# Bringing the solved 32x32 blocks back through DRAM in one load of 2 KB rows

## The chip, the cores and the metric

The kernel runs on one core of one Trainium2 chip. The metric is device time in microseconds (us). Three runs of the kernel before gave a median of 1629.85 us (1623.73 to 1634.08); a profiled execution stands beside them.

## The reference, cut to what matters

One layer of a decoder trunk is applied to a new sequence of 2048 positions and to 8 short samples of 8 positions. One input projection (1024 columns in) feeds two branches of 512 columns each, and one output projection joins them:

```
xn = rms_norm(x, norm_g);  p = xn @ w_in
conv branch : u = C*h;  z = 3-tap causal conv of u;  out = B * z * silu(G)
rwkv branch : per head (8 heads of 64), per token
    sa = S (-kk)
    S  = S * diag(w) + sa (kk*a)^T + v k^T
    o  = S r          then GroupNorm, + bonus, * silu(gate)
y = concat(conv, rwkv) @ w_out;  result = rms_norm(x + y)
```

The recurrence is computed in chunks of 64 positions. Inside a chunk the tokens depend on each other through a strictly triangular 64x64 matrix A, so each chunk and head needs (I - A)^-1. That inverse is the part this case is about.

## The kernel before, in words

**The outer loop.** Two halves of the sequence (`hf` 0 and 1, 1024 positions each; the samples ride with half 0) times four head pairs give eight passes, `s` = 0 to 7 (lines 925 to 956); I call them pair 0 to pair 7. One pass works on 128 partitions: two heads of 64. In program order a pass is `rwkv_pair` (four projection columns and the making of the recurrence's operands), `inverse`, `wkv` (16 chunks in order, with the group norm behind each block of 4, 6 and 6 chunks), and `conv_group` (four projection columns of the conv branch). Pass 3 differs: there `conv_group` and `xprep(1)`, which normalises and transposes the second half of the input, stand in the program ahead of `inverse` and `wkv` (lines 950 to 954).

**The order of the work.** No order is written by hand. Every tile is asked for by a tag, and tiles of one tag share a fixed number of buffers. When the kernel is compiled, a planner takes the operations in program order as their priority, puts each on its engine's queue as soon as its operands and its buffer are there by the planner's own durations, and fills the rest of each engine with later operations that are ready. The order on each engine is then fixed; on the chip an engine waits at its next instruction until its semaphores are there. So the projection matmuls (`pj`) of the conv group and of the next pair fill TensorE between the small matmuls of the recurrence.

**The inverse.** `rwkv_pair` leaves A in tile `AB`, `AB[128, chunks, 128]`, one tile for each of the three blocks. `store_blocks` (line 624) writes the diagonal 32x32 blocks to DRAM (`dn`), and `inverse` (line 636) reads them back as `na` with one block (head h, half b, chunk c) on a partition, twice: partitions 0 to 63 solve the even columns of each inverse block, 64 to 127 the odd ones. The tile `x` holds the columns, 16 a partition, 32 long. It has tag `xi`, one buffer, and is set to the identity by three memsets on GpSimd (lines 640 to 643). `subst` (line 610) solves on VectorE in 31 steps of two operations. Then `x` goes to DRAM (`dx`) in two stores (line 665), and comes back as matrices with 32 rows on partitions: for each of the three blocks, four loads (two heads by two diagonal blocks, line 674) write straight into the diagonal blocks of `AB`. Store and load move runs of 32 floats, 128 bytes. For each block the off-diagonal part follows (lines 676 to 690): a transpose on VectorE, small matmuls into `cx`, a copy split over ScalarE and VectorE, small matmuls again, and a copy into `AB`. After that `wkv` reads `AB` as an operand of its chunks (`ca`, `oo`).

**The tag `c2`.** It has four buffers of 2 KB a partition and serves short uses: in `sample_chunk` the state `s0` that is loaded from an input (line 803, passes 0 to 3) and four temporaries, in `wkv` the output block `ob`, in `gn_out` the tile `yo` that is stored to DRAM, and in `xprep(1)` the discarded output of the eight sums of squares on ScalarE (line 247, one for each of eight row tiles of the input).

**Queues.** SyncE (SP) issues the stores and loads of `dn`, `na`, `dx`, `AB`, of `yd` and of the weights in half 0; GpSimd's queue issues the weights in half 1 (`wh<-wsp`, `wl<-wsp`).

Of the kernel before, what the change touches and what calls it, by code (L numbers as in the profile page):

```python
# [8 lines left out]
F32 = mybir.dt.float32  # L9
# [78 lines left out]
def trunk_kernel(ctx, tc, I, O):  # L88
    nc = tc.nc
    act, dve, pe, pool, sync = nc.scalar, nc.vector, nc.tensor, nc.gpsimd, nc.sync  # L90
# [5 lines left out]
    dram = ctx.enter_context(tc.tile_pool(name="dram", bufs=1, space=DRAM))  # L96
    cnt = [0]

    def T(pool, shape, tag, bufs=1, dt=F32):
        cnt[0] += 1  # L100
        return pools[pool].tile(shape, dt, tag=tag, bufs=bufs, name=f"{tag}_{cnt[0]}")
# [8 lines left out]
    def CX(shape):  # L110
        return PS(shape, "cx", 1)
# [4 lines left out]
    def copy(out, in_, scale=1.0, bias=0.0):  # L116
        act.activation(out=out, in_=in_, func=AF.Copy, scale=scale, bias=bias)  # L117
# [7 lines left out]
    def mul(out, in0, in1):  # L125
        tt(out, in0, in1, ALU.mult)

    def mm(out, lhsT, rhs, start=True, stop=True):
        pe.matmul(out, lhsT=lhsT, rhs=rhs, start=start, stop=stop)  # L129
# [53 lines left out]
    for p in range(NPAIR):  # L183
        t = T("const", [128, 64], f"sst{p}")
# [425 lines left out]
    def subst(na, x, n, par):  # L610

        rows = na.shape[0]
        cw = x.shape[1]
        for s in range(n - 1):
            w = min(s // par + 1, cw)
            m = n - 1 - s
            t = T("small", [128, 144], "sub", 1)[:rows, :w * m].rearrange("p (c t) -> p c t", t=m)
            mul(t, x[:, 0:w, s:s + 1].to_broadcast([rows, w, m]),
                na[:, s, s + 1:n].unsqueeze(1).to_broadcast([rows, w, m]))
            tt(x[:, 0:w, s + 1:n], x[:, 0:w, s + 1:n], t, ALU.add)  # L620
            if s % 4 == 3:
                yield
# [13 lines left out]
    def inverse(S):  # L636
        cb = S.cb
        na = T("pair", [128, 32, 32], "na", 1)
        x = T("pair", [128, 16, 32], "xi", 1)
        pool.memset(x, 0.0)  # L640
        xf = x.rearrange("p c t -> p (c t)")
        for q in range(2):
            pool.memset(xf[q * 64:q * 64 + 64, q::34], 1.0)
        for q in range(2):
            sync.dma_start(out=na[q * 64:q * 64 + 64], in_=S.dn.rearrange("h b c s t -> (h b c) s t"))
        if cb:
            ab = S.AB[0][:, 0, 0:64]
            dd = T("small", [128, 8], "dd", 1)
            dve.tensor_reduce(out=dd, in_=ab.rearrange("p (b t) -> p t b", t=8), axis=mybir.AxisListType.X, op=ALU.add)
            nas = T("small", [16, 8, 8], "nas", 1)  # L650
            sync.dma_start(out=nas, in_=dd)
            xs_ = T("small", [16, 8, 8], "xis", 1)
            pool.memset(xs_, 0.0)
            pool.memset(xs_.rearrange("p c t -> p (c t)")[:, 0::9], 1.0)
            yield from subst(nas, xs_, 8, 1)
            d2 = T("small", [128, 8], "dd", 1)
            sync.dma_start(out=d2, in_=xs_)
            mul(ab.rearrange("p (b t) -> p b t", t=8), d2.unsqueeze(1).to_broadcast([128, 8, 8]),
                bmask.unsqueeze(2).to_broadcast([128, 8, 8]))
        yield from subst(na, x, 32, 2)  # L660
        yield
        cnt[0] += 1
        dx = dram.tile([2, 2, 16, 16, 2, 32], F32, tag="dx", bufs=2, name=f"dx_{cnt[0]}")
        for q in range(2):
            sync.dma_start(out=dx[:, :, :, :, q, :].rearrange("h b c s t -> (h b c) s t"), in_=x[q * 64:q * 64 + 64])
        ty = T("pair", [128, 2, 16, 32], "na", 1)
        t1, ys = ty[:, 0], ty[:, 1]
        for bl in S.bls:
            AB, n, c0_ = S.AB[bl.i], bl.nch, bl.ch0
            e = 1 if bl.samp else 0  # L670
            for h in range(2):
                for b in range(2):
                    r = h * 64 + b * 32
                    sync.dma_start(out=AB[r:r + 32, e:e + n, b * 32:b * 32 + 32],
                                   in_=dx[h, b, c0_:c0_ + n].rearrange("c s q t -> (s q) c t"))
            dve.transpose(out=t1[:, c0_:c0_ + n, :], in_=AB[:, e:e + n, 0:32])
            py = CX([128, n, 32])
            for c in range(n):
                for h in range(2):
                    a, b = h * 64, h * 64 + 32  # L680
                    mm(py[b:b + 32, c, :], AB[a:a + 32, e + c, 32:64], t1[a:a + 32, c0_ + c, :])
            copy(ys[32:64, c0_:c0_ + n], py[32:64])
            dve.tensor_copy(out=ys[96:128, c0_:c0_ + n], in_=py[96:128])
            pt = CX([128, n, 32])
            for c in range(n):
                for h in range(2):
                    a, b = h * 64, h * 64 + 32
                    mm(pt[a:a + 32, c, :], ys[b:b + 32, c0_ + c, :], AB[b:b + 32, e + c, 32:64])
            copy(AB[0:32, e:e + n, 32:64], pt[0:32])
            dve.tensor_copy(out=AB[64:96, e:e + n, 32:64], in_=pt[64:96])  # L690

# [234 lines left out]
    for s in range(8):  # L926
# [23 lines left out]
        if s == 3:  # L950
            run(conv_group(xs, hf, p))
            xs = xprep(1)
        run(inverse(S))
        wkv(S)
        if s != 3:
# [4 lines left out]
    for hf in range(2):  # L960
        for bl in half_blocks(hf):
            e = SAMP if bl.samp else 0
            for i in range(bl.np // 128):
                t = slice(hf * HALF + bl.p0 + i * 128, hf * HALF + bl.p0 + (i + 1) * 128)
# [58 lines left out]
```

## Time and profile before

| what | before |
|---|---|
| median of three runs | 1629.85 us (1623.73 to 1634.08) |
| the profiled execution | 1627.34 us, of it 1625.4 us from the first to the last instruction |
| busy | TensorE 93%, its weight loads 78%, VectorE 62%, ScalarE 38%, GpSimd 18% |
| mean granted clock of TensorE | 0.966 |
| DMA packets | 121967, of them 62617 under 512 bytes |
| chain that ended last | TensorE 63%, VectorE 22%, DMA 6% |

Busy shares are averages over the span; a matmul's end is modelled, so a busy TensorE is not one at its peak. The chain of waits is followed back from the last instruction: at each step to what released it, or to the instruction before it on its engine. The granted clock is 1.00 at 2.4 GHz and 0.50 at 1.2 GHz; a mean between them is a mixture of the two.

### The profile page before, as it was taken

What the parts mean: (1) busy time and instruction counts of PE and PEld (TensorE: products, weight loads), DVE (VectorE), ACT (ScalarE), POOL (GpSimd) and SP (SyncE); (2) the same over time, 40 slices, a digit from 0 to 9 for tenths busy, and PEclk for the clock granted to TensorE, in tenths of its full rate; (3) what the DMA queues carried; (4) which work ended last, traced back from release to release, by engine and by line L of the source; (5) the groups of instructions that cost most, each with busy time, mean ns of one, the idle gap of its engine ahead of it and who ended that gap; (6) DMA issues with size and microseconds to landing.
All of it is one profiled execution on the core that took longest, in us unless ns stands there. A gap on an engine that the chain in (4) does not pass through costs nothing.

```text
span 1625.4 us, 29341 instructions
## 1 busy us (share of the span) xinstructions
PE 1517.5 (93%) x11088; PEld 1267.9 (78%) x11088; DVE 1011.9 (62%) x3101; ACT 616.3 (38%) x1591; POOL 290.4 (18%) x395
## 2 busy tenths in 40 slices
PE   4999999989999999879999899999998999899997
PEld 4988877877788778867789678977896788667885
DVE  7387458655687458775587258635863587466544
ACT  6452345324532354344451245134413533342221
POOL 3133103311133112320022002200220022000000
PEclk9999999899999998989999899999999999899999
DMA  7323412242043213341123212321241135414441
GB/s 239 117 83 126 122 44 96 84 121 81 19 131 112 94 49 113 124 137 60 36 62 109 67 35 63 108 68 36 61 124 53 36 100 158 144 61 136 141 138 52
DMA packets 121967, 151.90 MB, mean 93 GB/s; under 512 B 62617, under 2 KB 86681, under 8 KB 121826
## 3 DMA queue, kind: packets, MB, share of 16 engines
q1 hardware_dynamic: 107024, 104.53, 20.9%
q0 software_dynamic: 9536, 34.64, 6.7%
q10 hardware_dynamic: 5266, 10.86, 1.8%
q8 instruction: 88, 1.44, 0.4%
q14 instruction: 53, 0.43, 0.1%
HBM read 92.60 MB, written 57.35 MB: 92 GB/s over the span
## 4 chain that ended last, share of the span: by engine, by line
PE 63%; DVE 22%; DMA 6%; issue 5%; ACT 3%; SPq 1%; POOL 1%; ACTq 0%; DVEq 0%; POOLq 0%
PE pj L129 41%; PE ca L129 5%; PE ax L129 5%; DVE sub L123 5%; DVE xi L123 4%; PE cb L129 4%; PE oo L129 2%; DVE hp L123 2%; PE cx L129 2%; PE cx L699 1%; DMA hp<-in_x_prompt 1%; DMA dx<-xi 1%; DVE hp L120 1%; DMA AB<-dx 1%; DMA na<-dn 1%
## 5 line engine op out<-in xcount | busy, mean ns | idle before, releaser
L129 PE MATMUL pj<-xh,wh 128*128 128x384 f32 (+3 forms) x1856 | 654.8, 353 | 17.4 <-DVE hp L123 13.7
L129 PE MATMUL pj<-xl,wh 128*128 128x384 f32 (+3 forms) x1856 | 652.6, 352 | 2.6 <-POOL xl L207 1.9
L129 PE MATMUL pj<-xh,wl 128*128 128x384 f32 (+3 forms) x1856 | 652.0, 351 | 0.6 <-DMA wl<-wsp 0.6
L129 PEld LDWEIGHTS pj<-xh,wh 128*128 128x128 f32 x1856 | 356.3, 192 | 50.1 <-DVE hp L123 11.2
L129 PEld LDWEIGHTS pj<-xl,wh 128*128 128x128 f32 x1856 | 356.8, 192 | 31.4 <-POOL xl L207 2.8
L129 PEld LDWEIGHTS pj<-xh,wl 128*128 128x128 f32 x1856 | 355.4, 191 | 28.1 <-issue 2.0
L117 ACT ACTIVATE tS<-sv,wc 64x64 f32<-64x64 f32 x256 | 88.0, 344 | 118.7 <-DVE sv L120 95.6
L207 POOL TENSOR_TENSOR wl<-wr,wh 128x512 fp32r<-128x512 f32 x66 | 87.6, 1338 | 195.1 <-ACT wh L117 191.7
L120 DVE SCALAR_TENSOR_TENSOR sv<-cb,wc,tS 64x64 f32<-64x64 f32 x240 | 68.0, 283 | 62.7 <-PE cb L129 55.0
L129 PE MATMUL ax<-L,bk 64*128 64x128 f32 x528 | 79.4, 299 | 21.0 <-DVE bk L123 12.7
L129 PEld LDWEIGHTS ax<-L,bk 64*128 64x128 f32 x528 | 66.3, 198 | 38.0 <-issue 23.2
L123 DVE TENSOR_TENSOR sub<-xi,na 128x126 f32<-128x126 f32 (+22 forms) x248 | 79.8, 322 | 16.3 <-DMA na<-dn 9.2
L117 ACT ACTIVATE t<-pj,prm 128x384 f32<-128x384 f32 (+3 forms) x170 | 68.9, 433 | 53.5 <-PE pj L129 52.4
L747 DVE TENSOR_SCALAR u<-ca,Q 128x64 f32<-128x64 f32 x128 | 36.2, 283 | 81.2 <-PE ca L129 81.0
L527 POOL TENSOR_TENSOR bk<-t,t 64x384 f32<-64x384 f32 (+2 forms) x56 | 58.0, 1036 | 144.4 <-ACT t L499 78.3
L123 DVE TENSOR_TENSOR xi<-xi,sub 128x126 f32<-128x126 f32 (+22 forms) x248 | 76.8, 310 | 7.3
L117 ACT ACTIVATE wh<-wr 128x512 fp32r<-128x512 f32 x66 | 40.5, 625 | 94.6 <-PE pj L129 74.5
L129 PEld LDWEIGHTS ca<-sv,L 128*64 128x64 f32 x528 | 43.7, 134 | 38.1 <-DVE sv L120 13.8
L737 DVE COPY xs<-ca 128x64 f32<-128x64 f32 x128 | 28.7, 224 | 66.2 <-PE ca L129 57.0
L129 PE MATMUL ca<-sv,L 128*64 128x64 f32 x528 | 68.7, 245 | 0.1
L294 POOL DMA_DIRECT2D wh<-wsp x33 | 18.7, 567 | 273.9 <-PE pj L129 199.6
L123 DVE TENSOR_TENSOR hp<-pj,hp 128x512 f32<-128x512 f32 (+1 forms) x34 | 23.4, 689 | 62.7 <-PE pj L129 62.3
(203 smaller groups left out, 2064.7 us busy)
## 6 DMA issues: line engine op xcount, KB each, us to landing
wr<-in_w_in SPq DMA_DIRECT2D x66, 256.0 KB, 3.7
wsp<-wh SPq DMA_DIRECT2D x33, 512.0 KB, 2.9
wsp<-wl SPq DMA_DIRECT2D x33, 512.0 KB, 3.9
wh<-wsp POOLq DMA_DIRECT2D x33, 512.0 KB, 3.6
wl<-wsp POOLq DMA_DIRECT2D x33, 512.0 KB, 4.5
hp<-in_x_prompt SPq DMA_DIRECT2D x29, 512.0 KB, 4.0
la<-yd SPq DMA_DIRECT2D x16, 512.0 KB, 4.0
out_y_p<-hp ACTq DMA_DIRECT2D x16, 512.0 KB, 2.6
```

The lines of the kernel that those rows point to most:

```text
L117: act.activation(out=out, in_=in_, func=AF.Copy, scale=scale, bias=bias)
L120: eng.scalar_tensor_tensor(out=out, in0=in0, scalar=scalar, in1=in1, op0=op0, op1=op1)
L123: dve.tensor_tensor(out=out, in0=in0, in1=in1, op=op)
L129: pe.matmul(out, lhsT=lhsT, rhs=rhs, start=start, stop=stop)
L207: eng.tensor_tensor(out=lo, in0=src, in1=hi.bitcast(F32), op=ALU.subtract)
L294: pool.dma_start(out=wh, in_=wsp[col, 0])
L527: pool.tensor_tensor(out=S.bk[bl.i][hs, chs, h, :], in0=ta[hs, a:a + n].rearrange("p (c j) -> p c j", j=64), in1=wi[hs, a:a + n].rearrange ...
L699: pe.transpose(out=pb[:, i, :], in_=S.bk[bi][:, ca + i].rearrange("p a t -> p (a t)"), identity=ident)
L737: dve.tensor_copy(out=xs_, in_=px)
L747: dve.tensor_scalar(out=u, in0=pu, scalar1=S.Q[:, q:q + 1], scalar2=None, op0=ALU.mult)
```

## The change

The solved columns are stored with another order of the axes, `[h, b, s, q, c, t]` in place of `[h, b, c, s, q, t]`, so that a row of the inverse is 16 chunks of 32 floats, 2 KB in one piece. The store is eight DMAs of 16 partitions each. One load brings all blocks of the pair into a new tile `xd` (tag `xd`, one buffer, the size of the old `xi`). Transposes and matmuls read `xd`; GpSimd and ScalarE copy the diagonal blocks from it into `AB`, two copies each for each block. The tile `x`, which had the tag `xi`, now takes one of the four buffers of `c2`.

```
     def inverse(S):
         cb = S.cb
         na = T("pair", [128, 32, 32], "na", 1)
-        x = T("pair", [128, 16, 32], "xi", 1)
+        x = T("ch", [128, 16, 32], "c2", 4)
...
-        dx = dram.tile([2, 2, 16, 16, 2, 32], F32, tag="dx", bufs=2, name=f"dx_{cnt[0]}")
+        dx = dram.tile([2, 2, 16, 2, 16, 32], F32, tag="dx", bufs=2, name=f"dx_{cnt[0]}")
         for q in range(2):
-            sync.dma_start(out=dx[:, :, :, :, q, :].rearrange("h b c s t -> (h b c) s t"), in_=x[q * 64:q * 64 + 64])
+            for h in range(2):
+                for b in range(2):
+                    u = q * 64 + (h * 2 + b) * 16
+                    sync.dma_start(out=dx[h, b, :, q].rearrange("s c t -> c s t"), in_=x[u:u + 16])
+        xd = T("pair", [128, 16, 32], "xd")
+        sync.dma_start(out=xd, in_=dx.rearrange("h b s q c t -> (h b s q) c t"))
...
-            for h in range(2):
-                for b in range(2):
-                    r = h * 64 + b * 32
-                    sync.dma_start(out=AB[r:r + 32, e:e + n, b * 32:b * 32 + 32],
-                                   in_=dx[h, b, c0_:c0_ + n].rearrange("c s q t -> (s q) c t"))
-            dve.transpose(out=t1[:, c0_:c0_ + n, :], in_=AB[:, e:e + n, 0:32])
+            cs = slice(c0_, c0_ + n)
+            dve.transpose(out=t1[:, cs, :], in_=xd[:, cs, :])
...
-                    mm(pt[a:a + 32, c, :], ys[b:b + 32, c0_ + c, :], AB[b:b + 32, e + c, 32:64])
+                    mm(pt[a:a + 32, c, :], ys[b:b + 32, c0_ + c, :], xd[b:b + 32, c0_ + c, :])
+            for h in range(2):
+                a = h * 64
+                pool.tensor_copy(out=AB[a:a + 32, e:e + n, 0:32], in_=xd[a:a + 32, cs, :])
+                copy(AB[a + 32:a + 64, e:e + n, 32:64], xd[a + 32:a + 64, cs, :])
             copy(AB[0:32, e:e + n, 32:64], pt[0:32])
             dve.tensor_copy(out=AB[64:96, e:e + n, 32:64], in_=pt[64:96])
```

## Rows read from the trace of the kernel before

**Rows 1.** The page: busy time of each engine, and the chain that ended last.
```profile
PE 1517.5 (93%) x11088; PEld 1267.9 (78%) x11088; DVE 1011.9 (62%) x3101; ACT 616.3 (38%) x1591; POOL 290.4 (18%) x395
...
PE 63%; DVE 22%; DMA 6%; issue 5%; ACT 3%; SPq 1%; POOL 1%; ACTq 0%; DVEq 0%; POOLq 0%
```

**Rows 2.** Windows: stretch, length, busy time by engine, granted clock, DMA share, GB/s.
```profile
1052.00:1212.00 160.00, 153.79 (x1224) 130.97 (x1223) 95.88 (x309) 57.54 (x157) 25.41 (x42) 0.97 0.24 69
700.00:720.00 20.00, 13.39 (x136) 11.55 (x136) 11.31 (x28) 10.36 (x19) 4.11 (x4) 0.83 0.73 195
720.00:760.00 40.00, 36.19 (x326) 28.47 (x326) 25.60 (x59) 22.61 (x63) 5.72 (x6) 0.91 0.13 41
760.00:823.00 63.00, 62.53 (x526) 48.42 (x526) 35.34 (x152) 29.32 (x88) 4.14 (x9) 1.00 0.13 40
890.00:921.00 31.00, 25.18 (x239) 21.53 (x238) 6.50 (x17) 6.41 (x20) 3.58 (x8) 0.78 0.32 77
```

**Rows 3.** Timeline of SP, pair 0: start us, length us, line, transfer, count.
```profile
164.75 1.30 SPq L665 DMA_DIRECT2D dx<-xi  x2
...
169.14 7.11 SPq L674 DMA_DIRECT2D AB<-dx  x12
```

**Rows 4.** Timeline of SP, pair 4.
```profile
889.85 1.26 SPq L665 DMA_DIRECT2D dx<-xi  x2
...
894.22 8.89 SPq L674 DMA_DIRECT2D AB<-dx  x12
```

**Rows 5.** Timeline of VectorE: the first transpose of pair 0 and of pair 4.
```profile
171.95 0.31 DVE L676 STREAM_TRANSPOSE na<-AB 128x128 f32<-128x128 f32 x1
...
901.79 0.31 DVE L676 STREAM_TRANSPOSE na<-AB 128x128 f32<-128x128 f32 x1 [0.49 <-DMA AB<-dx]
```

**Rows 6.** Waits of TensorE and GpSimd: who for whom, us in total, times, longest.
```profile
PE cx L129 <- DVE na L676: 17.4, 7, 5.8
...
POOL xi L640 <- DMA dx<-xi: 57.4, 5, 13.7
```

**Rows 7.** Instructions on tile AB: duration ns min/median/max, first and last start, forms.
```profile
L674 SPq DMA_DIRECT2D AB<-dx x96: 302/439/1920, 169.1 to 1388.0; - x96
...
L550 POOL TENSOR_TENSOR AB<-AB,Q x44: 288/507/617, 92.1 to 1338.6; 128x192 f32<-128x192 f32 x32, 128x256 f32<-128x256 f32 x8, 128x64 f32<-128x64 f32 x4
...
L117 ACT ACTIVATE AB<-cx x24: 254/319/322, 174.1 to 1398.7; 32x192 f32<-32x192 f32 x16, 32x128 f32<-32x128 f32 x8
```

**Rows 8.** The page: DMA issues, count, size of one, median us from issue to landing.
```profile
wr<-in_w_in SPq DMA_DIRECT2D x66, 256.0 KB, 3.7
...
dx<-xi SPq DMA_DIRECT2D x16, 128.0 KB, 3.5
...
AB<-dx SPq DMA_DIRECT2D x64, 24.0 KB, 2.0
```

**Rows 9.** Timeline of VectorE: the last write into c2 in pair 2.
```profile
628.37 0.59 DVE L120 SCALAR_TENSOR_TENSOR c<-c,prm,sg 128x384 f32<-128x384 f32 x1
```

**Rows 10.** Timeline of ScalarE: first and eighth square of xprep(1), the state's load of pair 3.
```profile
668.12 1.04 ACT L247 ACTIVATE c<-hp 128x1024 bf16<-128x1024 f32 x1
...
719.42 1.05 ACT L247 ACTIVATE c<-hp 128x1024 bf16<-128x1024 f32 x1
719.98 0.34 ACTq L803 DMA_DIRECT2D c<-in_state_wkv  x1
```

**Rows 11.** Groups of VectorE from 662 to 700 us: the solve of pair 3.
```profile
L123 DVE TENSOR_TENSOR xi<-xi,sub 128x126 f32<-128x126 f32 (+22 forms) x31 | 8.7, 280 | 0.8
L123 DVE TENSOR_TENSOR sub<-xi,na 128x126 f32<-128x126 f32 (+22 forms) x31 | 7.9, 254 | 0.8
```

**Rows 12.** Timeline of SP: the stores of the solved columns of pair 3.
```profile
699.10 1.29 SPq L665 DMA_DIRECT2D dx<-xi  x2
```

**Rows 13.** Timeline of VectorE: first chunk of pairs 0 and 3, last norm of pair 3.
```profile
196.56 0.28 DVE L747 TENSOR_SCALAR u<-ca,Q 128x64 f32<-128x64 f32 x1 [0.71 <-PE ca L129]
...
751.00 0.28 DVE L747 TENSOR_SCALAR u<-ca,Q 128x64 f32<-128x64 f32 x1 [0.69 <-PE ca L129]
...
822.90 0.62 DVE L120 SCALAR_TENSOR_TENSOR c<-c,prm,sg 128x384 f32<-128x384 f32 x1
```

**Rows 14.** Windows of the projection matmuls (pj) on TensorE alone: busy time, clock, DMA.
```profile
700.00:720.00 20.00, 6.20 (x48) 0.83 0.73 195
720.00:760.00 40.00, 23.03 (x87) 0.91 0.13 41
760.00:823.00 63.00, 42.49 (x189) 1.00 0.13 40
```

## The prediction, made before the changed kernel ran

> **What bounds the kernel now.** I read the page first. TensorE is busy 93% of the span, and the chain that ended last runs 63% over TensorE, 22% over VectorE and 6% over DMA [rows 1]. The windows say how these belong together: one whole period of half 1, from the stores of pair 5 to those of pair 6, lasts 160 us and TensorE is busy in 153.8 of them [rows 2]. Inside a period the recurrence is one serial chain (solve, DRAM, off-diagonal part, sixteen chunks, next pair's operands), and projection matmuls fill TensorE beside it. So a shortcut in the chain gains only what TensorE stands idle for, and a delay in the chain costs nothing until the filling runs out.
>
> The changed stretch shows where it is idle. In pair 0 the stores are issued at 164.75 us and the first transpose starts at 171.95, 7.2 us later [rows 3, 5]; in pair 4 it takes 11.9 us, from 889.85 to 901.79 [rows 4, 5]. The order on TensorE's queue is fixed, so where data come later than planned it stands: 17.4 us in 7 waits for the transposes, the longest 5.8 us [rows 6]. After that longest one the clock falls too, to a mean of 0.78 over 31 us [rows 2], which is 0.22 x 31 = 6.8 us of full-clock time. In quiet passes the stop is short or nothing.
>
> **The change part by part.**
>
> *Stores and load.* Before, SP issues 2 stores and 12 loads a pair. Afterwards it issues 8 stores and 1 load. A small transfer costs SP a median of 0.44 us [rows 7], but with the gaps 12 take 7.11 us or 0.59 each in pair 0 [rows 3]; I take 0.47 for a store (bounds 0.30 and 0.59). The eighth is issued 7 x 0.47 = 3.3 us behind the first and lands 2.0 us later, as the small loads do [rows 8], so 5.3 us after the first. The bounds are 2.1 + 2.0 and 4.1 + 3.5 (the big stores' landing). The load has the shape of a weight load, 256 KB in 2 KB rows, median 3.7 us to landing [rows 8]. Transposes can start at about 5.3 + 3.7 = 9.0 us. That is 1.8 us later than pair 0's 7.2 and 2.9 us earlier than pair 4's 11.9. What comes sooner is the second and third block: all three land together. But the three share one PSUM buffer (`cx`) and go one after the other anyway, so this helps only where a later load was late.
>
> By the Trainium skill (DMA: Bandwidth & Descriptors, "Anatomy of one DMA") a transfer takes about 2.0 us fixed plus its bytes at 436 GB/s, fitted on GpSimd's queue. For this load that is an estimate of 2.6 us where the row has 3.7; by it every operand would come 1.1 us sooner, up to 9 us over eight pairs.
>
> The loaded passes 4 to 6 gain at most the 17.4 us of waiting and the clock behind it, the quiet ones lose up to 1.8 us each. How the planner places the small matmuls anew the trace cannot show. If it moves them with the data, the stops vanish (17 us gained, and up to 7 more for the clock); if it leaves them where they are, all eight pairs stop for about 2 to 3 us, some 20 us in place of 17.4, with a part of the clock loss in the quiet passes too. I take +4 us; bounds -24 and +14. The value is near the second end, because the plan was short of the real transfers in the loaded passes before [rows 6] and SP's issue of eight stores is added ahead of the load.
>
> *SP's queue.* It is past the pair's transfers about 3 us sooner. Behind them wait stores of `yd`, a small weight tile and, in half 0, weights; TensorE does not wait for these by the list of waits, so nothing is gained.
>
> *Copies into AB.* Per block two on ScalarE, 32x192 like the copy from `cx`, 0.32 us each [rows 7]: 24 x 2 x 0.32 = 15 us of an engine that is 38% busy. They wait for the load alone and can go while TensorE makes the first product. If ScalarE takes them just ahead of the copy that TensorE waits for, 0.64 us a block come into the chain, at most 15 us in all if nothing covers them. The two on GpSimd are no longer than its 0.51 us for four times the partitions [rows 7]; the chunks that need them come more than 10 us later. I take 0.
>
> *The buffer of x.* The wait of GpSimd for the old `xi` buffer goes, 57.4 us in 5 waits [rows 6]. GpSimd is 18% busy, and behind its memset stand splits and weight DMAs of which TensorE waits for almost none: 0. What takes its place is more serious. `x` now queues for `c2`. I read from the trace that buffers of a tag are given in program order: pair 3's load of `s0`, which needs nothing but a free `c2` buffer, is issued at 719.98 us, right behind the eighth square of `xprep(1)` at 719.42 [rows 10], although after pair 2's last `yo` at 628.37 [rows 9] no one uses `c2` until the first square at 668.12. In pass 3 `xprep(1)` stands ahead of `inverse`, so there `x` has to come behind the eight squares as well. In the other passes what stands ahead of `x` is the previous pair's last `yo`, which ends before the next solve can begin: no cost.
>
> Before, pair 3's solve (62 operations, 16.6 us of VectorE) lay between 662 and 700 us [rows 11], its stores at 699.10 [rows 12]. It now starts at about 720 and lasts about 24 us beside the rest of `xprep(1)`: the stores go out at 744, **45 us later**. Not all of it arrives. Stores to first chunk took 31.8 us in pair 0 and 51.9 in pair 3 [rows 3, 12, 13], where `xprep(1)` lay in between; afterwards I take 32 + 2 = 34, so the first chunk is at 778 and not at 751.00, 27 us later. From there to the last norm it took 72 us [rows 13], with a projection matmul under way for 42.5 of 62.5 busy us of TensorE from 760 to 823 [rows 14, 2]. 324 projection matmuls ran from 700 to 823; three columns of pair 4, 216 of them, need nothing of pair 3's recurrence and will have gone ahead, so the chunks queue behind fewer. I take 10 us off (bounds 0 and 20) and 3 for the shorter remainder of pair 4: **+14 us**, bounds 0 and 30. It is a loss because TensorE, idle some 7 of 20 us from 700 to 720 already [rows 2], runs out of filling in that stretch.
>
> *Sum.* Against the profiled execution, 1627.3 us (2.5 below the median): 1627.3 + 14 + 4 + 0 = **1645 us**.
>
> **The rivals.**
>
> *A: the transfers decide (faster).* The 96 loads of 128-byte runs are what makes pairs 4 to 6 late, and one load of long rows ends that; the planner puts the matmuls where the data are, and pair 3 is covered by pair 4's projections. Gain: 17.4 us of stops, 6.8 us of clock in pair 4, 0.03 x 160 = 4.8 us in the period from pair 5 and the same again in pair 6 [rows 2, 6], 34 us at most; with the bulk of it 1602 us. For it: 11.9 against 7.2 us. Against it: the same two trips through DRAM remain, and the order of buffers.
>
> *B: no change.* Pair 4's columns and `xprep(1)` fill TensorE while pair 3 waits, and the stops move rather than go: 1627 us, give or take 9. For it: TensorE at 153.8 of 160 us. It decides if more than the 216 independent matmuls can go ahead; `v` and the gate of pair 4 write tiles that pair 3's chunks still read, which speaks against it.
>
> *C: the wait in pair 3 comes through whole.* Of the 45 us nothing is caught up behind the chunks, and the clock falls beside a half-empty TensorE: 1627 + 45 = 1672 us. Against it: 20 of them lay in `xprep(1)` already.
>
> *D: the planner takes `x` ahead of the squares.* Then the term of 14 is 0, and the result is A or B.
>
> **How the numbers follow.** Chances: my sum 0.57 (1634 to 1662), B 0.24, A 0.12, C 0.07; D is inside A and B. A change of 1%, 16 us, is about what a measurement of this kernel tells from no change, so the edges are 1614 and 1646, and my sum sits at the upper one. Of its 0.57 a little over 0.3 lie beyond, as its upper bounds are further off; with C that is 0.42 slower by over 1%. Faster is A, 0.12. Within 1% remain 0.46. The range from 1616 to 1668 leaves out A (0.12) and the end of C.
>
> **What would show it.** Right: in the trace afterwards pair 3's solve stands behind the eighth square, at about 720 us, its store near 744, and its first chunk near 778; pairs 0 to 2 make their first transpose about 9 us after the first store, and all three blocks' data are there at once; the waits of TensorE for transposes stay in the teens. Wrong: the solve of pair 3 ends near 700 as before (then D), or its delay is there and pair 4's stores are not later than before (then B); or the stops of pairs 4 to 6 and the low clock behind them are gone, with the span below 1614 (then A).

## The result, and the profile after

The changed kernel takes **1638.09 us** (median of 20 runs, 1629.73 to 1645.91); the kernel before, beside it, 1626.51 (20 runs, 1612.72 to 1636.12). The ratio is 1.0073, with a 95% interval of 1.0055 to 1.0091: slower, by less than 1%. The forecast was 1645. The profiled execution of after took 1632.51 us, 1630.7 of it span. All ratios here are of fast executions, and stage times are read from one profiled execution each, which in ring_alone below was a slow one and in half1_and_ring and two_stores_four_loads lies 17 and 11 us under the median.

The page of after, as [rows 1]: busy time by engine, and the chain that ended last.

```profile
PE 1528.8 (94%) x11088; PEld 1275.0 (78%) x11088; DVE 996.8 (61%) x3101; ACT 637.4 (39%) x1639; POOL 301.9 (19%) x443
...
PE 73%; DVE 16%; issue 4%; DMA 4%; ACT 2%; POOL 1%; SPq 0%; DVEq 0%; POOLq 0%; ACTq 0%
```

These averages hide nearly everything. I cut both spans at two points of the chain, the first store of the solved columns of pair 2 and that of pair 4, and counted for each stage, from all matmul and clock records, TensorE's time without a matmul and half of its time at 1.2 GHz, which is what a TensorE that is busy throughout loses by the lower clock (us, the last three columns after less before):

| stage | before | after | length | idle | half of the time at 1.2 GHz |
|---|---|---|---|---|---|
| start to pair 2's store | 517.9 | 533.1 | +15.2 | +3.7 | +10.2 |
| pair 2's to pair 4's store | 371.9 | 405.1 | +33.2 | +11.6 | +35.8 |
| pair 4's store to the end | 735.5 | 692.5 | -43.0 | -21.2 | -19.6 |
| sum | 1625.3 | 1630.7 | +5.4 | | |

So the change costs 48 us in one part and gives 43 back in another. The windows of half 1, first in the kernel before, from pair 4's store to the end (columns as in [rows 2]):

```profile
889.80:1625.30 735.50, 694.53 (x5026) 565.96 (x5025) 430.70 (x1384) 247.93 (x645) 82.44 (x125) 0.96 0.29 88
```

and after: one period, from pair 5's store to pair 6's, which answers to the 160.00 us of [rows 2]; then the same stage whole; last the stretch of pair 3's chunks.

```profile
1091.40:1240.20 148.80, 146.69 (x1212) 124.41 (x1211) 91.55 (x309) 60.36 (x164) 27.95 (x49) 1.00 0.25 73
938.20:1630.60 692.40, 672.74 (x5004) 547.61 (x5002) 417.04 (x1381) 257.49 (x667) 90.30 (x147) 0.99 0.31 93
788.60:850.00 61.40, 50.37 (x390) 33.40 (x383) 22.69 (x83) 19.50 (x60) 1.41 (x2) 0.50 0.02 8
```

The period is 11 us shorter, at a clock of 1.00. The wait of TensorE for transposes, 17.4 us in [rows 6] and 15.8 of them in half 1, is gone there: its longest waits from 938 us to the end of after are these (who for whom, us, times, longest).

```profile
PE pj L129 <- DVE t L120: 1.9, 2, 1.0
PE pj L129 <- DVE xl L207: 1.7, 2, 1.6
```

The stops did not go because the data come sooner. In pair 4 of after the first transpose starts 13.9 us after the first store, where it was 11.9 before [rows 4, 5], and in pairs 5 to 7 it is 16.1, 12.9 and 19.4 us where it was 8.9, 10.7 and 7.3:

```profile
938.17 4.06 SPq L668 DMA_DIRECT2D dx<-c  x8
...
952.11 0.82 DVE L677 STREAM_TRANSPOSE na<-xd 128x128 f32<-128x128 f32 x3
```

In between TensorE runs 97 projection matmuls without a gap, where before it ran 45 and stood for 5.8 us. After, then before (columns: PE, clock, DMA share, GB/s; of `pj` alone):

```profile
938.20:952.60 14.40, 14.40 (x97) 1.00 0.69 197
```

```profile
889.90:902.30 12.40, 6.43 (x45) 0.95 0.61 146
```

In pair 3 it goes the other way. ScalarE, GpSimd's queue of work, VectorE and SP of after, as [rows 10 to 13]: the eighth square, the load of `s0`, the memset of `x`, the solve's first operation, the stores and the first chunk.

```profile
732.36 1.05 ACT L247 ACTIVATE c<-hp 128x1024 bf16<-128x1024 f32 x1
...
734.65 0.33 ACTq L808 DMA_DIRECT2D c<-in_state_wkv  x1
```

```profile
728.06 0.53 POOL L640 MEMSET c<- 128x512 f32 x1
...
733.24 0.18 DVE L123 TENSOR_TENSOR sub<-c,na 128x31 f32<-128x31 f32 x1
...
765.76 3.79 SPq L668 DMA_DIRECT2D dx<-c  x8
...
810.38 0.28 DVE L752 TENSOR_SCALAR u<-ca,Q 128x64 f32<-128x64 f32 x1 [1.65 <-PE ca L129]
```

The memset at 728.06 shows that `x` had its buffer 4.3 us ahead of the eighth square; it does not wait for that square itself. The solve starts at 733 and not at 676 us, the stores go out at 765.8 and not at 699.1 [rows 12], the first chunk comes at 810.4 and not at 751.0 [rows 13]. Of the projection matmuls, which filled the chunks of pair 3 before (189 from 760 to 823), the windows of tile `pj` of after have 28 left for the stretch at 0.50, and more than before in pair 4's chunks (373 in 109.9 us against 289 in 103.4). After, then before (columns: PE, PEld, DVE, ACT, clock, DMA share, GB/s; of `pj` alone):

```profile
788.60:850.00 61.40, 14.06 (x28) 7.47 (x28) 1.10 (x2) 0.58 (x1) 0.50 0.02 8
938.20:1048.10 109.90, 75.54 (x373) 56.91 (x372) 7.26 (x13) 9.43 (x23) 1.00 0.21 64
```

```profile
760.00:823.00 63.00, 42.49 (x189) 29.20 (x189) 3.90 (x7) 5.33 (x14) 1.00 0.13 40
889.80:993.20 103.40, 65.81 (x289) 48.05 (x289) 7.27 (x13) 7.86 (x20) 0.93 0.19 50
```

In half 0 the new path is late. SP's timeline in pair 0 of after, as [rows 3], and VectorE's, as [rows 5]:

```profile
163.34 4.05 SPq L668 DMA_DIRECT2D dx<-c  x8
167.50 4.44 SPq L380 DMA_DIRECT2D yd<-hp  x3
172.03 0.38 SPq L435 DMA_DIRECT2D t<-in_w_da  x1
172.58 0.33 SPq L670 DMA_DIRECT2D xd<-dx  x1
```

```profile
177.90 0.62 DVE L120 SCALAR_TENSOR_TENSOR hp<-pj,omm,t 128x384 f32<-128x384 f32 x1 [3.47 <-ACT t L117]
178.44 0.82 DVE L677 STREAM_TRANSPOSE na<-xd 128x128 f32<-128x128 f32 x3
```

All three transposes stand together, 15.1 us after the first store (7.2 before). The load stands behind three stores of `yd`, and the transposes behind an operation on a projection, which waits for ScalarE: the planner has placed projections first. At the end of such a period TensorE's queue has no projection between 457.73 us and the first matmul on the next pair's operands, and TensorE stands until VectorE has made these; the next projections stand behind them in the queue. TensorE's timeline near 458 us in pair 1, where the granted clock is 0.50 for 17.1 us from 460.9:

```profile
457.73 0.33 PE L129 MATMUL pj<-xl,wh 128*128 128x384 f32 x1
461.59 0.76 PE L129 MATMUL ax<-L,bk 64*128 64x128 f32 x2 [3.54 <-DVE nwag L120]
...
463.14 0.69 PE L129 MATMUL pj<-xh,wl 128*128 128x384 f32 x1
```

Before, the longest stop ahead of such matmuls (`ax`) between the stores of pairs 0 and 3 was 1.5 us.

### The profile page after: what moved, and what is told of

Same layout as the page of the kernel before. It is cut to its first block, busy times and chain, and to the rows that moved or that the text cites. A ratio compares the mean times of both kernels' runs of the same rounds, so it can differ in the third digit from the quotient of the medians.

```text
span 1630.7 us, 29273 instructions
## 1 busy us (share of the span) xinstructions
PE 1528.8 (94%) x11088; PEld 1275.0 (78%) x11088; DVE 996.8 (61%) x3101; ACT 637.4 (39%) x1639; POOL 301.9 (19%) x443
## 3 DMA queue, kind: packets, MB, share of 16 engines
q1 hardware_dynamic: 91024, 104.53, 20.5%
## 4 chain that ended last, share of the span: by engine, by line
PE 73%; DVE 16%; issue 4%; DMA 4%; ACT 2%; POOL 1%; SPq 0%; DVEq 0%; POOLq 0%; ACTq 0%
PE pj L129 48%; PE ax L129 7%; PE ca L129 5%; PE cb L129 4%; DVE sub L123 3%; DVE c L123 3%; PE oo L129 2%; PE cx L129 2%; DMA na<-dn 2%; DVE hp L123 1%; PE cx L704 1%; DMA hp<-in_x_prompt 1%; DVE hp L120 1%; DVE bk L123 1%; PE cx L716 1%
## 5 line engine op out<-in xcount | busy, mean ns | idle before, releaser
L527 POOL TENSOR_TENSOR bk<-t,t 64x384 f32<-64x384 f32 (+2 forms) x56 | 53.3, 953 | 347.7 <-PE cb L129 105.5
L129 PE MATMUL ax<-L,bk 64*128 64x128 f32 x528 | 89.5, 317 | 21.5 <-DVE bk L123 7.9
L129 PEld LDWEIGHTS ax<-L,bk 64*128 64x128 f32 x528 | 71.2, 210 | 41.4 <-issue 25.6
L123 DVE TENSOR_TENSOR sub<-c,na 128x126 f32<-128x126 f32 (+22 forms) x248 | 78.9, 318 | 19.3 <-DMA na<-dn 12.2
L123 DVE TENSOR_TENSOR c<-c,sub 128x126 f32<-128x126 f32 (+22 forms) x248 | 75.0, 303 | 7.1
L120 DVE SCALAR_TENSOR_TENSOR hp<-pj,omm,t 128x384 f32<-128x384 f32 (+2 forms) x56 | 29.0, 529 | 76.6 <-ACT t L117 76.4
L129 PEld LDWEIGHTS ca<-sv,L 128*64 128x64 f32 x528 | 43.0, 140 | 40.7 <-DVE sv L120 15.2
L123 DVE TENSOR_TENSOR AB<-ax,msk 64x384 f32<-64x384 f32 (+2 forms) x88 | 48.7, 554 | 23.9 <-PE ax L129 22.7
```

What stands on the lines that cost most here:

```text
L120: eng.scalar_tensor_tensor(out=out, in0=in0, scalar=scalar, in1=in1, op0=op0, op1=op1)
L123: dve.tensor_tensor(out=out, in0=in0, in1=in1, op=op)
L527: pool.tensor_tensor(out=S.bk[bl.i][hs, chs, h, :], in0=ta[hs, a:a + n].rearrange("p (c j) -> p c j", j=64), in1=wi[hs, a:a + n].rearrange ...
```

## The experiments

A word on names: the **ring** is the four buffers of tag `c2`; the **path** is the new way through DRAM (stores, one load into `xd`, copies). Ratios are to the kernel before, run beside it.

**The path without the ring.** `xd` and `x` share the old single buffer.

```
-        x = T("ch", [128, 16, 32], "c2", 4)
+        x = T("pair", [128, 16, 32], "xi", 1)
...
-        xd = T("pair", [128, 16, 32], "xd")
+        xd = T("pair", [128, 16, 32], "xi", 1)
```

> The changed kernel, but x is taken out of the c2 ring: x and xd share one buffer (tag xi), which costs no memory, since xd is only loaded once x has been stored. Theory 1 (x behind the squares of xprep(1) costs the time, the new path itself gains in half 1): pair 3's solve starts near 676 us again and its first store is issued near 700, not at 766; the 61 us of half clock behind it are gone; pairs 4 to 7 keep the new, stop-free periods. Then 1595 to 1612 us, ratio to before 0.98 to 0.99. Theory 2 (the ring is innocent, the new transfers and the planner's order give and take about the same in each pass): 1630 to 1645 us, as the changed kernel.

1635.48 us, ratio 1.0058 (1.0026 to 1.0090). Pair 3's solve is back at 691 us, 15 us behind the kernel before, its first store goes out at 714, and there is no long stretch at 0.50; the time is no better. The ring alone does not explain the loss. Pair 3 has a new delay here: its eight stores stand between loads of the input on SP, the last one 14.5 us behind the first, the load is issued at 731.4, and the first transpose comes 28.3 us after the first store, where it was 15.0 before. By pair 4's store little of that is left: from pair 2's store to there it takes 373.2 us, 371.9 before.

**The ring without the path.** The kernel before with one line changed.

```
-        x = T("pair", [128, 16, 32], "xi", 1)
+        x = T("ch", [128, 16, 32], "c2", 4)
```

> The kernel before with one line of the change: x takes a buffer of c2, transfers and operands stay as before. Theory 1: pair 3's solve starts behind the eighth square, near 720 us or later, a long stretch at half clock follows, and pairs 4 to 6 keep their stops of 3 to 6 us at the transposes: 1645 to 1670 us, ratio 1.01 to 1.03. Theory 2: within 0.5% of before.

1653.58 us, ratio 1.0157 (1.0079 to 1.0235, four runs). The solve of pair 3 starts at 723.8 and the store is at 756.3 in this execution; in half1_and_ring below, whose half 0 is the same, at 712.1 and 744.6. So the ring in the kernel before does cost: more than the forecast's 14 us by the median, with the interval reaching from 13 to 38 us.

**The path with the ring, but `x` taken ahead of `xprep(1)`.** The allocation and the memsets become a function of their own, called in pass 3 ahead of the squares and elsewhere where they were.

```
+    def identity(S):
+        S.x = T("ch", [128, 16, 32], "c2", 4)
...
         if s == 3:
+            identity(S)
             run(conv_group(xs, hf, p))
             xs = xprep(1)
...
```

> The changed kernel, with x still in the c2 ring, but its allocation and its three memsets stand in the program ahead of xprep(1) in pass 3; in the other passes they stay where they are. Theory 1: the order of the ring in pass 3 is all that costs, so this is as fast as the kernel with its own buffer, 1595 to 1612 us, with pair 3's first store near 700 us. If the ring costs in every pass (x taking a quarter of c2 from the recurrence), the gain over the changed kernel is small and the time stays near 1635.

1636.63 us, ratio 1.0056 (1.0025 to 1.0087). The solve of pair 3 starts at 695.6 and its first store is at 718.3: that `x` stood behind the squares in program order was the cause of its delay. Undoing it brings nothing, as in the first experiment.

**Eight stores, but twelve loads straight into `AB`, no copies.** Own buffer; the layout of after.

```
+                    sync.dma_start(out=dx[h, b, :, q].rearrange("s c t -> c s t"), in_=x[u:u + 16])
...
+                                   in_=dx[h, b, :, :, c0_:c0_ + n].rearrange("s q c t -> (s q) c t"))
```

> x in its own buffer, the new order of the axes in DRAM and the eight stores, but the twelve loads as before, straight into AB (runs of 512 and 768 bytes in place of 128), without xd and without the copies. It parts the longer runs from the single load with copies. If the runs of 128 bytes are what made the loads of pairs 4 to 6 late, the transposes come 8 to 9 us after the first store in all pairs, TensorE's stops there go, and the time is 1595 to 1615 us. If the planner's place for the small matmuls decides, the stops stay at 10 us or more in total and the time is 1620 to 1635 us.

1643.51 us, ratio 1.0121 (1.0059 to 1.0184). Without the single load and the copies it is no faster, and slower than either range expected.

**Two stores and four loads.** Layout `[s, q, h, b, c, t]`, so that a store of 64 partitions is one DMA again; each load brings 32 rows of 2 KB; copies stay; own buffer.

```
+            sync.dma_start(out=dx[:, q].rearrange("s h b c t -> (h b c) s t"), in_=x[q * 64:q * 64 + 64])
...
+                sync.dma_start(out=xd[r:r + 32], in_=dx[:, :, h, b].rearrange("s q c t -> (s q) c t"))
```

> x in its own buffer as in own_buffer; the order of the axes in DRAM is [s, q, h, b, c, t], so that the store is two DMAs of 64 partitions again and xd comes back in four loads of 32 rows of 2 KB; xd and the copies stay. Theory 3 (the eight stores and the late load lengthen the chain in half 0, projections are spent ahead of the operand and lack behind the recurrence, where TensorE then stands 3.2 to 3.5 us and runs at half clock for 17): first transposes of pairs 0 to 2 come 8 to 10 us after the first store, not 13 to 15, the stops of 3.2 to 3.5 us near 276, 458 and 642 us go, and the time is 1610 to 1625 us. Theory 4 (the tile xd with its copies is what delays, whatever the stores): 1632 to 1640 us, as own_buffer.

1634.68 us, ratio 1.0062 (1.0026 to 1.0098), with first transposes 9.3, 8.4, 8.7 us after the store in pairs 0 to 2. With `xd`, the number of stores was not it. The late transposes are gone here and the stops for the next pair's operands are at most 2.5 us, yet the median is no better than own_buffer's: that these delays are what half 0 loses is not shown.

**Long runs alone.** The kernel before, with the same layout, two stores and twelve loads into `AB`: runs of 512 and 768 bytes in place of 128.

```
-                                   in_=dx[h, b, c0_:c0_ + n].rearrange("c s q t -> (s q) c t"))
+                                   in_=dx[:, :, h, b, c0_:c0_ + n].rearrange("s q c t -> (s q) c t"))
```

> The same DRAM order and two stores, but the twelve loads straight into AB, now runs of 512 and 768 bytes; no xd, no copies. Against the kernel before only the length of the loads' runs differs, against rows_direct only the number of stores. Theory 3: between 1615 and 1628 us, about 1% below rows_direct. If the runs of 128 bytes were what made the transposes of pairs 4 to 6 late, their stops shrink from 13.3 us to under 5 us in total; if they came late for another reason, the stops stay near 13 us.

1629.3 us, ratio 1.0024 (0.9995 to 1.0053); the DMA rows before, then here (KB of one, median us to landing):

```profile
AB<-dx SPq DMA_DIRECT2D x64, 24.0 KB, 2.0
AB<-dx SPq DMA_DIRECT2D x32, 16.0 KB, 2.9
```

```profile
AB<-dx SPq DMA_DIRECT2D x64, 24.0 KB, 2.1
AB<-dx SPq DMA_DIRECT2D x32, 16.0 KB, 3.0
```

The length of the runs is worth nothing that can be measured here. Against rows_direct only the number of stores differs, and with it the order of the outer axes in DRAM: 1.0024 against 1.0121, with intervals that do not overlap. So with twelve loads straight into `AB` the eight stores, or that order, do cost about 1%, as expected.

**The path in one half only.** The body of own_buffer stands under a condition, that of the kernel before in the other branch. This is half1_only; half0_only has `S.hf == 0`.

```
+        if S.hf == 1:
+            dx = dram.tile([2, 2, 16, 2, 16, 32], F32, tag="dx", bufs=2, name=f"dx_{cnt[0]}")
...
+        else:
+            dx = dram.tile([2, 2, 16, 16, 2, 32], F32, tag="dx", bufs=2, name=f"dx_{cnt[0]}")
...
```

> The new path (eight stores, one load, copies) in pairs 4 to 7 only, pairs 0 to 3 as before; x keeps its own buffer. Theory 1 (the path costs in half 0, where projections are put ahead of the operands, and gives some back in half 1): pair 4's first store within 3 us of the kernel before, then to the end some 724 us as in own_buffer in place of 735: 1610 to 1622 us, ratio 0.990 to 0.997. Rival (what the path costs is its copies and its load wherever it is used, and the shorter half 1 of own_buffer was only work done earlier): 1627 to 1636, ratio 1.000 to 1.006.

> The new path in pairs 0 to 3 only, pairs 4 to 7 as before; x keeps its own buffer. Theory 1: pair 4's first store 15 us later than before, as in own_buffer (905 in place of 890), stops of TensorE ahead of it for the next pair's operands of 3.2 to 3.5 us three times, and half 1 as before with its three stops: 1637 to 1645, ratio 1.006 to 1.011. Rival (the later pair 4 is paid for by projections done earlier, so that half 1 gets shorter all by itself): 1625 to 1631, ratio 0.999 to 1.003, pair 4's store to the end near 724.

Half 1 only: 1622.69 us, ratio 0.9976 (0.9949 to 1.0003). Half 0 only: 1641.57, ratio 1.0114 (1.0078 to 1.0150). The rival falls, in half0_only clearly (its store of pair 4 is at 909.5 and half 1 from there on takes 730.4 us, not 724), in half1_only by the median alone, as its interval reaches 1.0003; theory 1's gain there falls just short of what it expected. The path costs in half 0 and not in half 1. TensorE's waits in half0_only from 165 to 535 us show the stops seen above in after, in the last three lines; the first line is there before too (6.2 us in 4), and the longest wait for `bk` was 1.5 us:

```profile
PE pj L129 <- DVE hp L123: 6.3, 4, 2.6
PE ax L129 <- DVE bk L123: 4.6, 4, 2.2
PE ax L129 <- DVE nwag L120: 3.6, 1, 3.6
PE ax L129 <- DVE nwyg L120: 3.2, 1, 3.2
```

> As half1_only, but with two stores and four loads of 32 rows. Theory 1: 1610 to 1622, within 4 us of half1_only; first transposes 11 us after the store, as in two_stores_four_loads. Theory 'eight stores are what costs': at least 5 us faster than half1_only. Rival as for half1_only: 1627 to 1636.

With two stores and four loads in half 1 alone: 1621.48, ratio 0.9965 (0.9937 to 0.9993), 1.2 us beside half1_only. With `xd`, the theory of the eight stores falls.

**The copies alone.** two_stores_long_runs, with its loads into `xd` and the copies behind them.

```
-                    sync.dma_start(out=AB[r:r + 32, e:e + n, b * 32:b * 32 + 32],
+                    sync.dma_start(out=xd[r:r + 32, cs],
...
...
+                pool.tensor_copy(out=AB[a:a + 32, e:e + n, 0:32], in_=xd[a:a + 32, cs, :])
+                copy(AB[a + 32:a + 64, e:e + n, 32:64], xd[a + 32:a + 64, cs, :])
```

> two_stores_long_runs with one thing added: its twelve loads go into xd, and the copies bring the blocks into AB. Theory 'copies cost nothing' (the prediction's 0): ratio within 0.003 of two_stores_long_runs, 0.999 to 1.005. Theory 'the copies and the plan that they bring are the common part of what own_buffer and two_stores_four_loads lose': ratio 1.005 to 1.009, with pair 4's first store at 900 or later in place of 890.

1630.13, ratio 1.0029 (1.0000 to 1.0057), beside 1.0024 without the copies: they cost nothing that can be measured. What own_buffer and two_stores_four_loads have in common beyond this is that `xd` comes whole, in one load or four, in place of block by block. That they lose by it is not shown: the intervals of 1.0062 and 1.0029 overlap. rows_direct, where it doesn't, loses in another way: TensorE stops for the off-diagonal parts for 1.2 and 1.3 us in each of the pairs 0 to 2.

**The ring with the path in one half.** half1_only and half0_only, each with the line of ring_alone.

> half1_only with x in the ring of four buffers (tag c2) in all eight pairs. Theory 1 (pair 3's solve waits behind the eighth square and its store goes out some 57 to 66 us later, but with the new path in half 1 the projections that were done meanwhile let pairs 4 to 6 run without stops, so that the wait is paid back): half 1 from pair 4's first store to the end at 690 to 705 us, 1622 to 1630, ratio 0.996 to 1.002. Rival (the wait costs the 1.6% that it costs in ring_alone, whatever the path in half 1): 1640 to 1652, ratio 1.008 to 1.015. In both the solve of pair 3 starts behind the eighth square, at about 722.

> half0_only with x in the ring in all eight pairs: the new path in pairs 0 to 3, the old one in pairs 4 to 7. Theory 1 (it is the path in half 1 that pays the wait back): the losses of half0_only (1.0114) and of ring_alone (1.0157) stand beside each other, half 1 as before at 725 us or more with its stops for transposes, 1655 to 1675, ratio 1.018 to 1.028. Rival (the wait in pair 3 takes in what half 0 lost, as both are made up for by projections done earlier): 1636 to 1648, ratio 1.006 to 1.013.

Half 1 and ring: **1617.06 us, ratio 0.9948 (0.9911 to 0.9984)**, faster than both kernels, and than was expected. Half 0 and ring: 1675.37, ratio 1.0336 (1.0290 to 1.0383), above what was expected and, by the medians alone, more than the sum of the two losses. With these, all eight combinations have run:

| path in half 0 | path in half 1 | `x` in its own buffer | `x` in the ring |
|---|---|---|---|
| old | old | 1 (before) | 1.0157 |
| old | new | 0.9976 | 0.9948 |
| new | old | 1.0114 | 1.0336 |
| new | new | 1.0058 | 1.0073 (after) |

Half 1 from pair 4's store to the end, one window each: own_buffer, half0_and_ring, half1_and_ring.

```profile
905.40:1629.40 724.00, 693.13 (x5028) 560.48 (x5026) 428.29 (x1384) 257.98 (x669) 91.07 (x149) 0.98 0.29 89
```

```profile
943.20:1671.70 728.50, 688.57 (x5004) 561.00 (x5002) 429.21 (x1381) 246.92 (x643) 81.01 (x123) 0.96 0.29 88
```

```profile
905.40:1598.70 693.30, 672.14 (x5004) 547.19 (x5002) 416.32 (x1381) 257.34 (x667) 90.10 (x147) 0.99 0.31 93
```

Before it was 735.5. The path without the ring (own_buffer, half1_only) shortens this stage by 11 and 7 us, the ring with the old path in half 1 (half0_and_ring) by 7, or 2 against half0_only; both together by 42, as in after. One execution differs from the next by some us, but over all profiled kernels the groups stand apart: this stage takes 692.5 and 693.3 us in after and half1_and_ring, and 720 to 740 in all others; from pair 2's to pair 4's store it takes 392 to 409 us where `x` stands behind the squares, and 367 to 376 elsewhere; up to pair 2's store it takes 532 to 535 us with after's path in half 0 and 514 to 525 with that of before. x_before_xprep has the ring and the new path in half 1, but not the wait in pair 3, and takes 724.9: what goes with the gain is the wait, not the buffer. TensorE's longest waits in the windows of half0_and_ring and then half1_and_ring show what differs:

```profile
PE cx L129 <- DVE na L711: 11.3, 3, 5.4
PE ax L129 <- DVE bk L123: 3.7, 4, 1.3
```

```profile
PE pj L129 <- POOL xl L207: 2.6, 2, 1.8
PE pj L129 <- DVE t L120: 1.9, 2, 1.0
```

With the old path the stops for transposes stay although the ring is there. With both they are gone, and more projections stand beside pair 4's chunks. The windows of `pj` in pair 4's chunks: half0_and_ring, own_buffer, half1_and_ring.

```profile
943.20:1042.20 99.00, 64.33 (x306) 46.77 (x305) 6.61 (x12) 8.47 (x21) 1.00 0.23 66
```

```profile
905.40:1010.90 105.50, 69.89 (x341) 52.10 (x339) 7.85 (x14) 8.86 (x22) 1.00 0.22 65
```

```profile
905.40:1015.40 110.00, 75.64 (x373) 56.98 (x372) 7.29 (x13) 9.43 (x23) 1.00 0.20 63
```

306, 341 and 373 projection matmuls, 289 before, in windows of 99 to 110 us. The same count elsewhere in the run shows what became of the work. From pair 2's to pair 3's store, before and after (of `pj` alone; half1_and_ring has the same 792):

```profile
517.90:699.10 181.20, 125.70 (x598) 98.93 (x596) 13.42 (x30) 12.06 (x30) 0.97 0.30 96
```

```profile
533.10:765.80 232.70, 157.87 (x792) 132.37 (x791) 17.60 (x37) 16.47 (x42) 0.93 0.31 101
```

From pair 7's store to the end, before and after (half1_and_ring has the same 765):

```profile
1379.10:1625.30 246.20, 204.98 (x805) 147.31 (x803) 23.97 (x35) 0.00 (x0) 0.96 0.35 112
```

```profile
1406.20:1630.60 224.40, 191.04 (x765) 137.20 (x763) 22.05 (x32) 0.00 (x0) 0.99 0.33 106
```

While pair 3 waits, TensorE does 194 projection matmuls more, and behind the last pair's store 40 fewer are left. That last stretch is 22 us shorter, half of the 43 us that after gives back in half 1.

## Why the prediction was right or wrong

The total and the sign came out (1645 against 1638, within the range), but through terms that were each too small and that partly cancel: that the total lies near is luck. It was right in where the delay starts and wrong in what the path does.

- **Stores and load.** Eight stores took 4.05 us on SP in pair 0, the last issued 3.6 us behind the first, inside the bounds (0.30 to 0.59 each, 2.1 to 4.1 us for the last); in pairs 1 and 2 it is 4.8 and 4.4, outside. They land in a median of 1.9 us. For the load, the weight row's 3.7 us was too long: its median is 2.7 (2.5 to 4.3). The estimate of 2.6 us by the Trainium skill (DMA: Bandwidth & Descriptors, "Anatomy of one DMA") was nearer; for the weight rows, which are as large, it would say the same 2.6 where they show 3.7. The step that failed is "Transposes can start at about 5.3 + 3.7 = 9.0 us.": they start 12.7 to 15.1 us after the store in pairs 0 to 2. By the median the data are there at about 175.3 us in pair 0 (172.58 + 2.7); the transposes come at 178.44. The two steps left out were SP's `yd` stores ahead of the load, and the planner's projections ahead of the transposes.
- **The term of +4 us for the path** had the wrong form. It took all eight pairs as alike. half0_only and half1_only show +1.14% and -0.24%, about +19 and -4 us (the second with an interval that reaches 1.0003); beside the ring, half 1's part is -2.1% (0.9948 against 1.0157). "If it moves them with the data, the stops vanish (17 us gained, and up to 7 more for the clock)" is what came to pass in half 1 beside the ring, with 43 us gained in place of 24: the time without a matmul fell by 21 and the clock gave back 20, not 7, since not only pair 4 had run at 1.2 GHz behind its stops. The data are not sooner there but later, and projections stand ahead of the matmuls that need them (97 in place of 45 in pair 4).
- **The ring's order** was right, and x_before_xprep shows it: the solve starts behind the eighth square (732.36, then 733.24) in after, and at 695.6 when `x` was taken ahead of the squares. That it waits for the eighth square was not right: `x` is set at 728.06, and the row it was read from (719.42, then 719.98) has the load issued while that square still runs. Sizes: solve at 733 for 720, store 66.7 us later for 45, first chunk 59 us later for 27. About 13 us of each are half 0's loss, which shifts the squares themselves (719.42 to 732.36); without it, in half1_and_ring, the store goes out at 744.6, for 744, by a solve that starts 8 us sooner than forecast and takes 8 us longer. The solve took 32.5 us, forecast 24; from store to first chunk it was 44.6 us, forecast 34.
- **"The chunks queue behind fewer"** was right in kind: 28 projection matmuls are left from 788.6 to 850. The forecast took this as a gain of 10 us and did not price its other side: in that stretch, with few projections between the small matmuls, TensorE was granted 1.2 GHz throughout, where [rows 2] has 1.00. Rather than catching up, pair 3 fell further behind: from the first chunk to the last norm (810.38 to 897.73) it took 87.4 us and not 72.
- **The term of +14 us** stands for +33 us between pair 2's and pair 4's stores (+20 in the profiled execution of half1_and_ring). That alone it would make the change 2% slower; it does in the kernel before (ring_alone, +1.6%) and with the path in half 0 (1.0336 against 1.0114). With the path in half 1 it costs nothing: 0.9948 against 0.9976, and 1.0073 against 1.0058. The forecast had no term for this interaction. The wait is given back later: TensorE does 194 projection matmuls more during it, and half 1 runs without stops. That the one makes room for the other is a reading of the counts; ring_alone has the same 194 and keeps its stops.
- **Copies** at nothing: right, by their own experiment. That GpSimd's wait for the buffer of `x` is worth nothing was not tried by itself.
- **The rivals.** A (the transfers decide) is right for half 1 only, and for another reason than long rows: two_stores_long_runs keeps the waits for transposes (15.8 us in 5 from 890 us on, as before), and in after the transposes of pairs 4 to 7 come later, not sooner. C's price, 45 us, is nearly the +48 us by pair 4's store; it did not last to the end. The mark set for B (pair 4's stores not later) failed: they are 48 us later. The mark set for the forecast, "the waits of TensorE for transposes stay in the teens", failed too.

What stays open: why the planner finds the plan without stops only with both the wait in pair 3 and the path in half 1. The counts of `pj` show that it does, not by which of its rules. Also open is what half 0 loses by. SP's order and the projections placed ahead delay the transposes there, but two_stores_four_loads, where they come 8 to 9 us after the store, loses as much in all by its median.

## What to carry to other kernels

A change to one transfer in a kernel that is ordered by a planner is two changes: the transfer, and a new plan. Price the first from rows, but test the second by cutting the change in space (one half, one pass) and by crossing its parts, since here two parts that cost 1.1% and 1.6% alone came with a third that is worth 0.2 to 2.6%, depending on its company. A new user of a shared tag waits for whoever stands ahead of it in program order: look for the pass where that order differs. The version to keep here is the new path in half 1, with the ring by the median (0.9948); half1_four_loads (0.9965) and half1_only (0.9976) lie within its interval.

## What the runs showed of the hardware that was not expected

- The length of the contiguous runs in these small loads made no difference: 128 bytes or 512 to 768 bytes, landing 2.0 and 2.1 us for 24 KB, ratio 1.0024 (0.9995 to 1.0053). By the Trainium skill (DMA: Bandwidth & Descriptors, "Specifications") 512 bytes is the least for the full rate; nothing of that is seen at this size.
- TensorE ran at 1.2 GHz for 61.4 us on end in pair 3 of after, though no stop in it was longer than 1.3 us: ahead of the fall it stood for 0.8 to 1.1 us between the groups of the off-diagonal product. Before, with projections between them (526 matmuls from 760 to 823, 189 of them projections [rows 2, 14]), the same chunks ran at 2.4 GHz. In the other kernels in which `x` stands behind the squares the stretch is 75.1 us (ring_alone, half0_and_ring) and 27.3 us (half1_and_ring); elsewhere no stretch in pair 3 is longer than 20.5 us.
- Single stops of 3.2, 3.5 and 3.5 us in half 0 of after came with 10.2, 17.1 and 17.1 us at 1.2 GHz, which begin 2.0 us behind the end of the first stop and 0.7 and 1.7 us ahead of the end of the others. Half of each stretch is more than the stop itself.
